# Gate rows of the background conditioning: sum over partitions by one GpSimd instruction instead of four TensorE products

## The chip, the cores and the metric

The kernel runs on one core of a Trainium2 chip. A core has four compute engines that work side by side, each through its own queue in order: TensorE (PE, matrix products into PSUM), VectorE (DVE), ScalarE (ACT) and GpSimd (POOL); a fifth, SyncE (SP), issues the DMA transfers here. The metric is the device time of one execution in microseconds. The kernel before took 2260.77 us (median of three runs, 2260.18 to 2261.73).

## What is computed

Two layers of a diffusion backbone on 256 latent tokens of width 2048, with 256 context tokens beside them in the first layer. Every layer takes six modulation vectors from the conditioning vector c, and two of these are gates:

```python
def ada_mods(cvec, w, b):
    m = jax.nn.silu(cvec) @ w + b          # w is 2048 x 12288
    return jnp.split(m, N_MOD, axis=-1)    # shift, scale, gate; shift, scale, gate

hl = modulate(rms_norm(x, g_norm_mix[layer]), sh1, sc1)
yl = even_mixer(hl, ...) or pool_mixer(hl, ...)
x = x + gt1[:, None, :] * yl
x = x + gt2[:, None, :] * sq_relu_mlp(modulate(rms_norm(x, g_norm_ffn[layer]), sh2, sc2), w_up, w_down)
```

Everything is in float32. A gate multiplies whole columns of an output whose rows (tokens) lie on the 128 partitions, so it must stand in a tile of 128 equal rows.

## The kernel before

The work is a chain of large products: input projections and a gated linear attention with a chunk mixer (the even layer, up to about 550 us), an output projection, a feed-forward of 8192 columns (from about 660 us), a pooling layer (about 1400 to 1545 us) and the second feed-forward. Float32 products are made of parts that TensorE takes at speed: load_w (line 171) loads 1 MB of weights into raw, and for each 1024 columns ScalarE rounds them to hi (line 184) and VectorE makes the rest, lo = raw - hi (line 185), with three buffers each. The groups mma, mmb and mmf multiply hi and lo with the two parts of the activations, xt.

Beside this chain runs the conditioning, in the background. A comp is one vector of 2048 numbers, made by two tasks of 1024 columns each (ada, line 343; ada_task, line 294). A task is 16 chunks: a chunk loads 512 KB of w_ada to araw (line 308), and VectorE adds it, times its number of silu(c), onto acc (line 312), so that acc holds 128 partial sums a column, one in each partition. first (line 299) clears acc by a memset on GpSimd and loads the bias into row 0. last (line 316) sums over the partitions. It splits acc into two parts hi and lo, and then there are two cases. For a shift or scale, products with one-hot columns give rows of numbers, which are transposed to columns. For a gate (row is true), the products with a 128x128 matrix of ones give the sum in every partition at once, 512 columns at a time, and ScalarE copies them from PSUM to the gate tile (line 327). Ten comps, twenty tasks, four gates: eight tasks take the second case.

Chunks are put on a list, bg; pump (line 190) is called after each weight load and takes chunks from it at a rate that plan sets, at a priority below the chain's; need empties the list up to a comp that is now wanted. The tiles acc, araw and the parts share one ring of seven buffers (tag a4, 4 KB a partition). The scheduler of the framework writes each engine's order ahead of time from priorities and its own costs; on the chip each engine follows that order and waits where something isn't ready. GpSimd runs nothing but memsets and the powers of rstd (line 291). The gate tiles of the first gate lie in the ring g4, the others in a pool of four (gate_tile, line 215); residual (line 402) and grow read them.

Of the kernel before, what the change touches and what calls it, by code (L numbers as in the profile page):

```python
# [19 lines left out]
P = 128  # L20
# [130 lines left out]
class Builder:  # L151
# [142 lines left out]
    def ada_task(self, task, dst, row):  # L294

        nc = self.nc
        st = {}

        def first():
            st["acc"] = self.ap.tile([P, 1024], F32, tag="a4", bufs=NA4, name="acc")  # L300
            nc.gpsimd.memset(st["acc"], 0.0)
            nc.sync.dma_start(st["acc"][0:1, :], self.I["bada"][task:task + 1, :])

        def chunk(c):
            if c == 0:
                first()
            raw = self.ap.tile([P, 1024], F32, tag="a4", bufs=NA4, name="araw")
            nc.sync.dma_start(raw, self.I["wada"][task * 16 + c])
            acc = st["acc"]

            with self.tc.issue_after(self.norm) if self.norm is not None else nullcontext():
                nc.vector.scalar_tensor_tensor(acc, raw, self.csil[:, c, 0:1], acc, ALU.mult, ALU.add)  # L312
            if c == KT - 1:
                last()

        def last():
            hi, lo = (self.ap.tile([P, 1024], F32R, tag="a4", bufs=NA4, name="apart") for _ in range(2))
            nc.scalar.copy(hi, st["acc"])
            nc.vector.tensor_sub(lo, st["acc"], hi.bitcast(F32))
            if row:  # L320
                g = self.gate_tile()
                dst.append(g)
                for j in range(2):
                    ps = self.pa.tile([P, 512], F32, tag="ax", name="ps_ada")
                    for i, z in enumerate((hi, lo)):
                        self.mm(ps, self.ones, z[:, 512 * j:512 * j + 512], i == 0, i == 1)
                    nc.scalar.copy(g[:, 512 * j:512 * j + 512], ps)
            else:
                ps = self.pa.tile([P, 512], F32, tag="ax", name="ps_ada")
                rows = self.cp.tile([4, T], F32, tag="crow", bufs=1, name="crow")  # L330
                for j in range(4):
                    for i, z in enumerate((hi, lo)):
                        self.mm(ps[0:4, 0:T], self.hot[:, j], z[:, T * j:T * j + T], j + i == 0, j + i == 4)
                nc.scalar.copy(rows, ps[0:4, 0:T])
                for h in range(2):
                    nc.tensor.transpose(ps[:, T + 4 * h:T + 4 * h + 4], rows[:, h * P:h * P + P], self.ident[0:4, 0:4])
                nc.scalar.copy(dst.rearrange("p (j h) -> p h j", h=2), ps[:, T:T + 8].rearrange("p (h j) -> p h j", h=2))

        for c in range(KT):
            self.bg.append((task // 2, lambda c=c: chunk(c)))  # L340
# [814 lines left out]
```

## Time and profile before

| | us |
|---|---|
| median of three runs | 2260.77 |
| profiled execution, whole | 2260.99 |
| its span, first to last instruction | 2258.9 |
| TensorE busy | 2234.0 (99%) |
| VectorE busy | 1684.9 (75%) |
| ScalarE busy | 1103.0 (49%) |
| GpSimd busy | 36.6 (2%) |

The page shows one profiled execution. Busy time is the time in which an engine had an instruction in work; matmuls overlap, so that the sum of their durations is more than TensorE's busy time, and the step from the start of one to the start of the next tells what one takes. A group of instructions has its count, its busy time, its mean duration, and the idle time of its engine just before it with what ended that idle time. Idle time of an engine that others don't wait for costs nothing.

### The profile page before, as it was taken

The page shows a single profiled execution, that of the slowest core. Times are in us where ns is not written, and L with a number is a line of the kernel's source. Part 1 is how long each engine was busy: PE and PEld are TensorE (multiplying, and loading weights), DVE is VectorE, ACT ScalarE, POOL GpSimd, SP SyncE. Part 2 cuts the span into 40 slices and gives each one's busy share as a digit, 9 for nine tenths or more (in the row PEclk, how much of TensorE's full clock was granted, in tenths as well). Part 3 has the DMA queues.
Part 4 walks back from the last instruction along what each step waited for, and adds up shares of the span by engine and source line. Part 5 has one row for each costly group of instructions (what it writes and reads, how often), then busy time and mean ns, then how long its engine had stood idle before and what let it go on. Part 6 is the DMA issues. An engine that isn't in the chain of part 4 may idle for free. (4 is left out here: it accounts for less than half of the span.)

```text
span 2258.9 us, 31641 instructions
## 1 busy us (share of the span) xinstructions
PE 2234.0 (99%) x12532; PEld 1858.7 (82%) x12532; DVE 1684.9 (75%) x2055; ACT 1103.0 (49%) x1484; POOL 36.6 (2%) x47
## 2 busy tenths in 40 slices
PE   9999999999999999999999999999999999999998
PEld 5677787788888888888888888888888888888887
DVE  5669999998869877787888875769855655556655
ACT  4326466555436545544544545445444444443443
POOL 0000000000000000000000000000000000000000
PEclk9999999999999999999999999999999999999999
DMA  9786776788877888888888875646865555555553
GB/s 384 276 302 220 273 257 241 274 298 299 320 263 285 311 321 304 295 326 311 314 320 316 305 286 207 215 176 248 303 235 193 186 189 199 186 191 186 188 193 122
DMA packets 110636, 582.71 MB, mean 258 GB/s; under 512 B 12292, under 2 KB 12420, under 8 KB 66584
## 3 DMA queue, kind: packets, MB, share of 16 engines
q1 hardware_dynamic: 110488, 580.70, 70.8%
q8 instruction: 98, 1.61, 0.3%
q14 instruction: 50, 0.41, 0.0%
HBM read 578.55 MB, written 2.10 MB: 257 GB/s over the span
## 5 line engine op out<-in xcount | busy, mean ns | idle before, releaser
L184 ACT CAST hi<-raw 128x1024 fp32r<-128x1024 f32 (+1 forms) x701 | 732.9, 1046 | 926.2 <-PE mma L221 463.1
L185 DVE TENSOR_TENSOR lo<-raw,hi 128x1024 fp32r<-128x1024 f32 (+1 forms) x701 | 848.8, 1214 | 410.6 <-ACT hi L184 408.7
L221 PE MATMUL mma<-hi,xt 128*128 128x512 f32 x2800 | 871.5, 390 | 0.1
L221 PE MATMUL mmb<-xt,hi 128*128 128x512 f32 x2304 | 727.3, 396 | 1.1 <-DVE xt L390 0.8
L221 PEld LDWEIGHTS mma<-hi,xt 128*128 128x128 f32 x2800 | 524.6, 188 | 111.0 <-DVE q L281 0.5
L221 PE MATMUL mma<-lo,xt 128*128 128x512 f32 x1400 | 546.2, 390 | 0.8 <-DVE lo L185 0.8
L221 PEld LDWEIGHTS mmb<-xt,lo 128*128 128x128 f32 x2304 | 432.5, 188 | 103.5 <-DVE lo L185 2.5
L221 PE MATMUL mmb<-xt,lo 128*128 128x256 f32 x2304 | 455.0, 278 | 1.4 <-DVE lo L185 1.4
L312 DVE SCALAR_TENSOR_TENSOR acc<-araw,csil,acc 128x1024 f32<-128x1024 f32 x320 | 409.1, 1278 | 49.5 <-DMA araw<-in_wada 47.9
L221 PEld LDWEIGHTS mmb<-xt,hi 128*128 128x128 f32 x2304 | 352.7, 189 | 3.3 <-DVE xt L390 1.0
L221 PEld LDWEIGHTS mma<-lo,xt 128*128 128x128 f32 x1400 | 262.9, 188 | 57.1 <-DVE lo L185 1.5
L221 PE MATMUL mmf<-xt,hi 128*128 128x512 f32 x512 | 165.4, 395 | 0.6 <-ACT fbacc L602 0.5
L221 PEld LDWEIGHTS mmf<-xt,hi 128*128 128x128 f32 x512 | 96.1, 188 | 21.5 <-ACT fbacc L602 0.9
L221 PE MATMUL mmf<-xt,lo 128*128 128x512 f32 x256 | 100.2, 392 | 0.0
L221 PE MATMUL mmn<-hi,xt 128*128 128x256 f32 x416 | 76.0, 283 | 0.0
L221 PEld LDWEIGHTS mmn<-hi,xt 128*128 128x128 f32 x416 | 65.2, 192 | 0.4
L221 PE MATMUL mmn<-lo,xt 128*128 128x256 f32 x208 | 58.9, 283 | 0.0
L221 PEld LDWEIGHTS mmf<-xt,lo 128*128 128x128 f32 x256 | 48.2, 188 | 9.4
L741 ACT COPY both<-kk 128x256 f32<-128x256 f32 x64 | 26.4, 412 | 48.3 <-DVE kk L759 40.2
L390 DVE TENSOR_TENSOR xt<-hup,xt 128x512 fp32r<-128x512 f32 x64 | 43.8, 685 | 6.7 <-ACT xt L389 6.7
L604 DVE TENSOR_TENSOR fbacc<-mmf,fbacc 128x1024 f32<-128x1024 f32 x24 | 29.3, 1220 | 22.0 <-PE mmf L221 21.9
L221 PE MATMUL mmi<-hi,xt 128*128 128x512 f32 x128 | 44.2, 404 | 1.2 <-DVE xt L569 0.6
(187 smaller groups left out, 1341.0 us busy)
## 6 DMA issues: line engine op xcount, KB each, us to landing
araw<-in_wada SPq DMA_DIRECT2D x320, 512.0 KB
raw<-in_w_up SPq DMA_DIRECT2D x128, 1024.0 KB
raw<-in_w_down SPq DMA_DIRECT2D x128, 1024.0 KB
sraw<-in_wada_s SPq DMA_DIRECT2D x56, 512.0 KB
raw<-in_w_out SPq DMA_DIRECT2D x16, 1024.0 KB
raw<-in_w_pool SPq DMA_DIRECT2D x16, 1024.0 KB
raw<-in_w_fb SPq DMA_DIRECT2D x10, 1024.0 KB
raw<-in_w_q SPq DMA_DIRECT2D x8, 1024.0 KB
```

Of the source, the lines that this page charges most:

```text
L184: nc.scalar.copy(hi, raw[:, o:o + w])
L185: nc.vector.tensor_sub(lo, raw[:, o:o + w], hi.bitcast(F32))
L221: self.first_mm = self.nc.tensor.matmul(out, lhsT, rhs, start=start, stop=stop, **kw).ins
L312: nc.vector.scalar_tensor_tensor(acc, raw, self.csil[:, c, 0:1], acc, ALU.mult, ALU.add)
L390: return self.nc.vector.tensor_sub(x[:, :, lo], src, x[:, :, hi].bitcast(F32))
L604: nc.vector.tensor_add(fbacc[h], ps, fbacc[h])
L741: nc.scalar.copy(o.rearrange("p (s j i) -> p j s i", j=2, i=hh), bass.AP(src.tensor, src.offset, [list(src.ap[0]), [st + hh, 2], [seg, ns] ...
```

## The change

In last, a gate's task no longer splits acc and multiplies it with ones. One GpSimd instruction reads acc (128 partitions, 1024 columns), sums over the partitions and writes the sum to all 128 partitions of the gate tile. Shifts and scales are made as before.

```diff
@@ -314,6 +314,11 @@
                 last()
 
         def last():
+            if row:
+                g = self.gate_tile()
+                dst.append(g)
+                nc.gpsimd.partition_all_reduce(g, st["acc"], P, bass.bass_isa.ReduceOp.add)
+                return
             hi, lo = (self.ap.tile([P, 1024], F32R, tag="a4", bufs=NA4, name="apart") for _ in range(2))
             nc.scalar.copy(hi, st["acc"])
             nc.vector.tensor_sub(lo, st["acc"], hi.bitcast(F32))
```

The scheduler writes new orders for all engines. On GpSimd's queue, in the even layer, the piece around the first two gate tasks reads as follows (+ is new, - is gone; acc is the sum tile of a task, orr and vrr are results of rstd, ISA gate<-acc is the new instruction, and ISA alone an entry without operands):

```order
 L301 MEMSET acc 128x1024 x4
+L320 ISA
+L320 ISA gate<-acc 128x1024
+L301 MEMSET acc 128x1024
+L320 ISA gate<-acc 128x1024
+L291 ISA
 L291 TENSOR_TENSOR orr<-oms,mhalf 128x8
-L301 MEMSET acc 128x1024 x3
+L301 MEMSET acc 128x1024 x2
 L291 TENSOR_TENSOR vrr<-vms,mhalf 128x8 x2
```

The memset of the next task stands ahead of a task's sum over partitions, and that of the task after next behind it.

On VectorE's queue, at the end of the first task of the second gate (in the feed-forward of layer 0), the order before was this; the first L312 ends one task's acc, and the pair further down begins the next one's:

```order
L185 TENSOR_TENSOR lo<-raw_7905,hi 128x1024
L312 SCALAR_TENSOR_TENSOR acc<-araw,csil,acc 128x1024
L185 TENSOR_TENSOR lo<-raw_7905,hi 128x1024
L319 TENSOR_TENSOR apart<-acc,apart 128x1024
L185 TENSOR_TENSOR lo<-raw,hi 128x1024 x2
L185 TENSOR_TENSOR lo<-raw_7981,hi 128x1024 x2
L185 TENSOR_TENSOR lo<-raw,hi 128x1024
L312 SCALAR_TENSOR_TENSOR acc<-araw,csil,acc 128x1024 x2
```

Now it is this, at the same place of VectorE's queue:

```order
L185 TENSOR_TENSOR lo<-raw_7883,hi 128x1024
L312 SCALAR_TENSOR_TENSOR acc<-araw,csil,acc 128x1024
L185 TENSOR_TENSOR lo<-raw_7883,hi 128x1024
L185 TENSOR_TENSOR lo<-raw,hi 128x1024 x2
L185 TENSOR_TENSOR lo<-raw_7959,hi 128x1024
L312 SCALAR_TENSOR_TENSOR acc<-araw,csil,acc 128x1024 x2
L185 TENSOR_TENSOR lo<-raw_7959,hi 128x1024
L185 TENSOR_TENSOR lo<-raw,hi 128x1024
L312 SCALAR_TENSOR_TENSOR acc<-araw,csil,acc 128x1024 x2
```

The subtraction of acc is gone, and the next task's additions stand two instructions nearer to the end of this one.

On SyncE's queue the loads behind the same place now read so; what an entry waits for stands in brackets, and Pool_49 is GpSimd's semaphore:

```order
L174 DMA raw_8061<-in_w_up 128x2048 [waits DVE_49]
L308 DMA araw<-in_wada 128x1024 [waits DMAHW2_49]
L308 DMA araw<-in_wada 128x1024 [waits DMAHW4_49,DMAHW3_49]
L174 DMA raw<-in_w_up 128x2048 [waits DVE_49]
L308 DMA araw<-in_wada 128x1024 [waits DMAHW6_49,DMAHW5_49]
L308 DMA araw<-in_wada 128x1024 [waits Pool_49]
L174 DMA raw_8184<-in_w_up 128x2048 [waits DMAHW7_49,DVE_49]
```

The load of the next task's fourth chunk takes the buffer of acc and so waits for GpSimd, ahead of the weights of raw_8184; there are seven such loads behind gate tasks in the whole queue.

## Rows read from the trace of the kernel before

**Rows 1.** Page, span and part 1: busy us (share of the span) xinstructions.

```profile
span 2258.9 us, 31641 instructions
PE 2234.0 (99%) x12532; PEld 1858.7 (82%) x12532; DVE 1684.9 (75%) x2055; ACT 1103.0 (49%) x1484; POOL 36.6 (2%) x47
```

**Rows 2.** Waits of TensorE's matmuls: us in total, times, longest us.

```profile
PE mmb L221 <- DVE lo L185: 1.4, 2, 0.9
```

**Rows 3.** Page, part 5: line, engine, group, busy us, mean ns, idle before.

```profile
L184 ACT CAST hi<-raw 128x1024 fp32r<-128x1024 f32 (+1 forms) x701 | 732.9, 1046 | 926.2 <-PE mma L221 463.1
L185 DVE TENSOR_TENSOR lo<-raw,hi 128x1024 fp32r<-128x1024 f32 (+1 forms) x701 | 848.8, 1214 | 410.6 <-ACT hi L184 408.7
...
L312 DVE SCALAR_TENSOR_TENSOR acc<-araw,csil,acc 128x1024 f32<-128x1024 f32 x320 | 409.1, 1278 | 49.5 <-DMA araw<-in_wada 47.9
```

**Rows 4.** Timeline, second feed-forward: start us, us, engine, line, operation.

```profile
1976.21 1.05 ACT L184 CAST hi<-raw 128x1024 fp32r<-128x1024 f32 x1 [1.25 <-PE mmb L221]
...
1977.30 1.23 DVE L185 TENSOR_TENSOR lo<-raw,hi 128x1024 fp32r<-128x1024 f32 x1 [0.23 <-ACT hi L184]
...
1981.84 1.05 ACT L184 CAST hi<-raw 128x1024 fp32r<-128x1024 f32 x1 [1.75 <-PE mmb L221]
...
1984.60 1.09 PE L221 MATMUL ps_ada<-apart,ones 128*128 128x512 f32 x4
...
1985.53 0.40 PE L221 MATMUL mma<-hi,xt 128*128 128x512 f32 x1
```

**Rows 5.** Tiles apart and gate: ns min/median/max, first and last start us.

```profile
L221 PE MATMUL ps_ada<-apart,ones x32: 388/392/403, 339.0 to 1985.3; 128*128 128x512 f32 x32
L318 ACT CAST apart<-acc x20: 1046/1053/1058, 211.7 to 1652.7; 128x1024 fp32r<-128x1024 f32 x20
L319 DVE TENSOR_TENSOR apart<-acc,apart x20: 1210/1218/1227, 213.0 to 1653.8; 128x1024 fp32r<-128x1024 f32 x20
...
L414 DVE TENSOR_TENSOR rtmp<-mma,gate x24: 678/683/693, 606.6 to 2227.9; 128x512 f32<-128x512 f32 x24
L327 ACT COPY gate<-ps_ada x16: 569/587/599, 339.9 to 1986.5; 128x512 f32<-128x512 f32 x16
```

**Rows 6.** GpSimd's groups, shapes apart: busy us, mean ns, idle before.

```profile
L301 POOL MEMSET acc<- 128x1024 f32 x20 | 19.1, 956 | 1139.9 <-DVE acc L312 904.7 <-PE ps_as L221 120.9 <-DMA araw<-in_wada 114.3
L291 POOL TENSOR_TENSOR vrr<-vms,mhalf 128x8 f32<-128x8 f32 x2 | 5.3, 2636 | 48.6 <-DVE vms L839 26.8 <-DVE oms L804 21.8
...
L291 POOL TENSOR_TENSOR orr<-oms,mhalf 128x8 f32<-128x8 f32 x2 | 3.3, 1638 | 61.5 <-DVE oms L804 61.5
```

**Rows 7.** Timeline of GpSimd and VectorE, 495 to 500 us.

```profile
496.35 1.28 DVE L312 SCALAR_TENSOR_TENSOR acc<-araw,csil,acc 128x1024 f32<-128x1024 f32 x1
...
496.47 2.66 POOL L291 TENSOR_TENSOR vrr<-vms,mhalf 128x8 f32<-128x8 f32 x1 [26.80 <-DVE vms L839]
...
497.55 1.23 DVE L185 TENSOR_TENSOR lo<-raw,hi 128x1024 fp32r<-128x1024 f32 x1
```

**Rows 8.** Stretches: length; PE, PEld, DVE, ACT, POOL busy; PEclk, DMA share, GB/s.

```profile
130.00:550.00 420.00, 412.83 (x2963) 331.94 (x2963) 386.20 (x702) 230.47 (x413) 16.10 (x12) 1.00 0.73 267
660.00:1400.00 740.00, 737.67 (x3902) 628.24 (x3902) 587.77 (x557) 379.02 (x461) 10.69 (x12) 1.00 0.82 297
```

**Rows 9.** Timeline: additions to acc on VectorE, one pair of loads on SyncE.

```profile
308.89 1.27 DVE L312 SCALAR_TENSOR_TENSOR acc<-araw,csil,acc 128x1024 f32<-128x1024 f32 x1
...
849.96 1.28 DVE L312 SCALAR_TENSOR_TENSOR acc<-araw,csil,acc 128x1024 f32<-128x1024 f32 x1 [2.21 <-DMA araw<-in_wada]
...
865.29 1.65 SPq L308 DMA_DIRECT2D araw<-in_wada  x2
...
871.37 1.28 DVE L312 SCALAR_TENSOR_TENSOR acc<-araw,csil,acc 128x1024 f32<-128x1024 f32 x1 [0.51 <-DMA araw<-in_wada]
...
919.18 1.28 DVE L312 SCALAR_TENSOR_TENSOR acc<-araw,csil,acc 128x1024 f32<-128x1024 f32 x1
...
949.00 1.28 DVE L312 SCALAR_TENSOR_TENSOR acc<-araw,csil,acc 128x1024 f32<-128x1024 f32 x1
```

## The prediction

> **What bounds the kernel now.** I read the summary of the engines first. TensorE is busy for 2234.0 of 2258.9 us, and VectorE for three quarters of the span [rows 1]. A busy TensorE could still be one that is often kept waiting for a moment, so the list of its waits comes next: its matmuls waited for a split weight half (lo) 1.4 us in all in the group that waited longest for one [rows 2]. The groups show the other side: ScalarE, which writes the hi halves, sat idle for 926 us before them and was let go mostly by TensorE [rows 3]. So weights are ready ahead of TensorE nearly everywhere, and the end moves with TensorE's own instructions, one for one, as long as VectorE and the loads keep their lead. How large that lead is decides this case.
>
> **The lead of the weights.** A loaded weight tile is split in parts of 1024 columns, hi by ScalarE and then lo by VectorE, with three buffers each. In the feed-forward stage a hi begins every 2.8 us (two steps from 1976.21 to 1981.84) [rows 4], each time when TensorE lets a buffer go. Two other parts are then still ahead of it, so TensorE wants this part near 1976.2 + 2 x 2.8 = 1981.8. Its lo is finished at 1977.30 + 1.23 = 1978.5 [rows 4]. VectorE may therefore be late by 3.3 us before TensorE stands still.
>
> **What is removed.** Eight tasks make a gate half each. Each loses four products with the matrix of ones, one cast, one subtraction and two copies out of PSUM: in all 32 matmuls, 8 of the 20 casts, 8 of the 20 subtractions and 16 copies [rows 5]. A matmul has a duration of 392 ns, but they overlap; what one takes from TensorE is the step to the next. Four begin from 1984.60 on and the next product begins at 1985.53, so a step is 0.233 us [rows 4], and 32 x 0.233 = 7.4 us. They stand between matmuls that hardly wait, so all 7.4 us are on the path. VectorE loses 8 x 1.22 = 9.8 us and ScalarE 8 x 1.05 + 16 x 0.59 = 17.8 us [rows 5]; both were ahead, so I count nothing for them. Two buffers of the ring of seven (the hi and lo of acc) are no longer taken; one, acc itself, is held while the reduce runs.
>
> **What is added: eight reduces on GpSimd.** No row shows one. From below, one pass that reads and one that writes 128x1024, each at the price of a memset of that size, 0.956 us: 1.9 us [rows 6]. From above, a power on 8 columns takes 1.638 us, 0.205 us a column [rows 6], so 1024 columns would take 210 us. Between these far ends I take the memset, since adding is nearer to a pass than to a power: 128 partitions are seven halvings, at one pass each 7 x 0.956 = 6.7 us, at a read and a write each 13.4 us. I take 6.7 us and keep 13.4 us for the range. The Trainium skill, page "GPSIMD Engine Reference", section 3.2, gives 247.7 us for a different cross-partition reduction of [128, 2048]; half of it, an estimate of 124 us, would make the kernel slower by hundreds of microseconds (the last rival). No run here shows it so far.
>
> **What runs beside them.** GpSimd is idle for nearly the whole span [rows 1]: its own time costs nothing by itself. But the reduce reads SBUF while VectorE does, and the trace has two places where such a pair meets. The power vrr takes 2.66 us at 496.47, when VectorE has just begun an accumulation of 1.28 us with two inputs from SBUF (496.35) [rows 7]; the two vrr take 2.636 us in the mean, and orr, of the same shape, 1.638 us [rows 6]. So GpSimd waited about 1.0 us, until VectorE's instruction was over, and got in before the next one; the lo at 497.55 kept its 1.23 us [rows 7], but there GpSimd had only eight columns to read. One side waits for the other, then, for an instruction at a time. With 1024 columns to read I expect the other side of it: the next VectorE instruction with two SBUF inputs, and all behind it in VectorE's queue, stands still until the reading is over. In the order of the changed kernel that is at once a lo, since four of them follow the last accumulation of a task. The rule stands in the Trainium skill, page "SBUF — State Buffer", section "Who interferes with whom": the pair of ports that the two share is locked by whoever comes first, for its whole instruction, also against a VectorE instruction with two SBUF inputs. The trace agrees for the half that it shows, GpSimd's 1.0 us; with the rule the sum is the one below, without it that of the first rival.
>
> Let the hold be h = 6.7 us. In the six feed-forward cases VectorE is 79% busy (587.77 of 740 us) [rows 8]. The first lo caught would on average have begun half a part, 1.4 us, after the hold began, and I put 0.5 us of other work before it: late by h - 1.4 + 0.5 = 5.8 us, less the lead of 3.3: TensorE stands for 2.5 us, six times 15.0. In the two cases of the even layer VectorE is 92% busy (386.20 of 420 us) [rows 8]; there I take the lo as due at once and 0.7 us of work before it: h + 0.7 - 3.3 = 4.1 us, twice 8.2. Together 23.2 us, or in general 8h - 30.4.
>
> **Queues.** GpSimd's queue gets six entries without operands (three at line 320, three at line 291), which I read as changes of the program that it runs. No row prices one. Each stands where GpSimd has nothing due for some 10 us: the first directly behind the memset for the second gate task, which the first task's last additions don't wait for, and what comes next, the sum of the first, is ready only at 308.89 + 1.27 = 310.2 [rows 9]. I cost them at nothing; a long one would cost what it exceeds that gap by. Behind a reduce stands the memset of the task after next, wanted after a whole further task. On SyncE's queue one load now waits for the reduce, since it takes over the buffer of acc, and weight loads queue behind it: tightest for the fourth chunk behind the task that ends at 849.96 + 1.28 = 851.2 [rows 9]. Loads land 4.8 us after issue (the second of the pair from 865.29 begins near 866.6, its sum at 871.37) [rows 9], and in the new order its sum comes near 866, by four lo's at the pace of 2.8 us and three sums: a reduce over 10 us makes VectorE wait, one over 13 us (the lead) TensorE too. At 6.7 us: nothing. The gates are wanted later: the first use of any is at 606.6 [rows 5], some 300 us after the first task's sum.
>
> **The sum**, against the profiled execution, 2260.99 us (2258.9 of span and 2.1 around it, 0.2 above the median of the runs): 2260.99 - 7.4 + 23.2 = 2276.8, said as 2277 us. In general 2260.99 + 8h - 37.8: it breaks even at h = 4.7 us, and ends at 2330 with 13.4 us. A measurement of this kernel can tell about 0.2%, 4.5 us, from no change; slower by that needs an h of 5.3 us.
>
> **Rivals.** *Faster: GpSimd gives way.* If the reduce reads in short pieces between VectorE's instructions, VectorE keeps its pace and only the 7.4 us count: 2253.6 us. For it: the lo of 1.23 us beside a running power [rows 7]. The reduce is then stretched: lo and accumulation take 848.8 + 409.1 = 1257.9 of 2258.9 us, 56% [rows 3], so 6.7 becomes 6.7 / 0.44 = 15 us, which at the one tight load costs 15 - 13 = 2 us: 2255.6. This side wins below a hold of 4.7 us. I give it 0.33, with 2251 to 2258 us. *Much slower: a slow reduce.* At a price per column like the power's, 210 us, loads behind seven of the eight wait. The usual slack is that of the sixth chunk behind: from 919.18 + 1.28 = 920.5 to 949.00 [rows 9], less 4.8 to land, plus the lead, 27 us. That makes 7 x (210 - 27) = 1281 us more, some 3535 us with the 7.4 off. Against it: a power is the dearest thing that GpSimd does here. By the Trainium skill's figure, page "GPSIMD Engine Reference", 124 us as an estimate, the same sum would give 7 x 97 = 679 us more. I give it 0.05.
>
> **How the numbers follow.** The forecast has 0.62, and its own range is 2262 to 2300 us (h from 4.9 to 9.6). Of it 0.48 lies above 0.2% slower, 0.09 within and 0.05 faster; of the first rival 0.24 is faster, 0.06 the same, 0.03 slower; the last is slower. That is faster 0.29, same 0.15, slower 0.56. The range runs from 2251 (the first rival, with a microsecond or two more from shorter queues) to 2300; left out are the slow reduce, 0.05, holds above 9.6 us, about 0.1, and a little below.
>
> **What would show it.** Eight GpSimd instructions that write gate, of 5 to 10 us. If I am right, at each of them one VectorE instruction with two SBUF inputs is longer than its 1.2 us by several microseconds, or has a gap before it, and the next matmuls wait for lo by 2 to 4 us; TensorE's waits for lo grow from a few us to some 20. If lo keeps 1.22 us there and TensorE has no new gaps, the first rival holds. A load of araw that waits past 10 us for a gate shows the stretched reduce. Wrong altogether I would be if the program changes held up rstd at a layer's start, or if the 32 matmuls had covered work that now comes late.

## The result, and the profile after

The changed kernel takes 2273.88 us (median of five runs, 2272.46 to 2276.08) where the kernel before takes 2260.77 beside it: a ratio of 1.006, with an interval of 1.005 to 1.0071. It is slower by 13 us. The forecast was 2277. The number is nearly right, but two of its terms are wrong by some 10 us each, in opposite directions, and that is what the experiments are about.

The page of the changed kernel, span and part 1, against [rows 1]:

```profile
span 2274.3 us, 31571 instructions
PE 2235.9 (98%) x12500; PEld 1856.3 (82%) x12500; DVE 1702.6 (75%) x2047; ACT 1088.7 (48%) x1460; POOL 90.9 (4%) x55
```

This profiled execution took 2276.08 us as a whole, so 15.1 us more than that of before. TensorE has 32 matmuls less and is busy for longer; VectorE has eight instructions less and is busy for 18 us longer. Part 5 of the page (busy us, mean ns, idle before) shows where VectorE's comes from, against [rows 3], and what the new instruction takes:

```profile
L185 DVE TENSOR_TENSOR lo<-raw,hi 128x1024 fp32r<-128x1024 f32 (+1 forms) x701 | 868.6, 1244 | 387.2 <-ACT hi L184 382.0
...
L312 DVE SCALAR_TENSOR_TENSOR acc<-araw,csil,acc 128x1024 f32<-128x1024 f32 x320 | 417.5, 1305 | 71.9 <-DMA araw<-in_wada 70.4
...
L320 POOL PARTITION_ALL_REDUCE gate<-acc x8 | 56.2, 7024 | 167.9 <-DVE acc L312 152.7
```

A reduce takes 7.02 us; the forecast had 6.7. The same 701 lo and the same 320 accumulations are 28.2 us longer in all. The means hide how: the view of the tile lo (duration in ns, least, median and most) has the same median as before, and a longest one of 5551.

```profile
L185 DVE TENSOR_TENSOR lo<-raw,hi x701: 679/1224/5551, 23.6 to 2258.4; 128x1024 fp32r<-128x1024 f32 x173, 128x512 fp32r<-128x512 f32 x3
```

The timeline of the changed kernel around the first reduce, in the even layer (start us, us, engine, line, operation, and in brackets the idle time before and what ended it):

```profile
310.24 6.49 POOL L320 PARTITION_ALL_REDUCE gate<-acc  x1 [15.29 <-DVE kk L764]
...
310.66 5.55 DVE L312 SCALAR_TENSOR_TENSOR acc<-araw,csil,acc 128x1024 f32<-128x1024 f32 x1
316.13 0.28 DVE L764 TENSOR_TENSOR kk<-kk,pyr 128x128 f32<-128x128 f32 x1
...
318.04 0.41 ACT L746 COPY both<-kk 128x256 f32<-128x256 f32 x1 [5.81 <-DVE kk L764]
...
320.81 0.43 PE L221 MATMUL ps_sc<-both 128*32 128x64 f32 x16 [3.80 <-ACT both L746]
...
867.89 6.92 POOL L320 PARTITION_ALL_REDUCE gate<-acc  x1 [9.01 <-DVE acc L312]
...
869.68 4.62 DVE L185 TENSOR_TENSOR lo<-raw,hi 128x1024 fp32r<-128x1024 f32 x1 [0.86 <-ACT hi L184]
```

An accumulation of 1.27 us takes 5.55. The small multiplications kk and qg behind it in VectorE's queue wait, ScalarE's copy waits for kk for 5.81 us, and TensorE stands for 3.80 us before the small matmul ps_sc. In the feed-forward stage (the last two rows) a lo is caught in the same way, 4.62 us for 1.22, and no matmul there waits for long. The list of TensorE's waits (us in total, times, longest) says the same of the whole execution:

```profile
PE ps_o L221 <- ACT st L788: 6.4, 6, 4.5
PE ps_sc L221 <- ACT both L746: 5.1, 5, 3.8
PE ps_mx L221 <- issue: 3.7, 1, 3.7
...
PE mma L221 <- DVE lo L185: 1.9, 4, 0.7
PE mmb L221 <- DVE lo L185: 1.8, 4, 0.5
```

The waits for lo are 3.7 us in all now, not some 20; before they were 2.2 (1.4 in mmb [rows 2] and 0.8 in mma). The new waits are those of the even layer's small matmuls. Where TensorE stands there, its granted clock falls behind it. In the stretches of 5 us (length, busy us of PE, PEld, DVE, ACT, POOL, then the granted clock) it is 0.70 behind the first reduce and 0.50 at 510 us, as means of the two levels, 1.2 and 2.4 GHz; the kernel before has 1.00 throughout 130 to 550 us [rows 8]. A mean of 0.70 over 5 us is 3 us at the lower level. Counted in this way the changed kernel spends 3.4 us there behind each of the first two reduces and 6.8 us from 510 us on, and at the lower level the same product takes twice the time. That is how TensorE can be busy for longer with 32 products less.

```profile
315.00:320.00 5.00, 2.00 (x86) 1.42 (x84) 5.00 (x11) 0.71 (x2) 1.73 (x1) 1.00 0.46 134
320.00:325.00 5.00, 4.19 (x47) 3.63 (x47) 5.00 (x11) 4.96 (x9) 0.00 (x0) 0.70 0.89 342
...
510.00:515.00 5.00, 3.85 (x11) 3.31 (x12) 3.28 (x9) 1.05 (x1) 0.67 (x1) 0.50 0.85 349
515.00:520.00 5.00, 5.00 (x26) 4.34 (x26) 3.81 (x7) 0.56 (x1) 0.00 (x0) 0.84 0.61 221
```

**Where the time came from.** Every kernel here makes 701 hi casts, so the n-th cast of one can be set against the n-th of another. The table gives how much later than in the kernel before the cast that stood at 298.6, 490.6, 608.6, 1179.9 and 2230.1 us began (from the timelines of the profiled executions). The first two steps are the even layer, the last two the rest with its feed-forward stages. The kernels below the first row are those of the next section.

| kernel | 298.6 | 490.6 | 608.6 | 1179.9 | 2230.1 |
|---|---|---|---|---|---|
| changed | -0.2 | 6.9 | 17.4 | 17.4 | 15.3 |
| e1, gate 0 on TensorE | 0.2 | -0.3 | -0.2 | -2.2 | -4.2 |
| e2, gate 0 alone on GpSimd | 0.3 | 8.8 | 13.5 | 13.9 | 13.1 |
| e3, no reading | 1.0 | -1.3 | 3.0 | -2.0 | -3.6 |
| e4, reduces twice | 0.3 | 18.3 | 25.2 | 39.5 | 45.0 |
| e5, pieces | 0.1 | 6.0 | 10.3 | 5.4 | 3.6 |
| e6, gate 0 later | -0.1 | 8.9 | 12.2 | 10.1 | 8.5 |
| e7, gate 0 on TensorE, rest in pieces | 1.1 | 0.3 | 0.3 | -3.3 | -6.2 |
| e8, as e7, no reading | 0.0 | 0.0 | 0.1 | -4.8 | -7.7 |
| e9, gate 0 put off | 2.5 | -0.9 | 14.9 | 10.2 | 8.7 |
| e10, put off, behind the memset | 0.8 | -1.5 | 7.5 | 3.1 | 2.4 |

Each row is one execution, and a median differs from it by up to 3.5 us (the changed kernel was profiled at 2276.08 for a median of 2273.88, e1 at 2256.89 for 2260.36, e5 at 2264.32 for 2267.02, e6 at 2269.19 for 2272.65). A difference of 2 or 3 us between two rows is a hint and not a proof.

The changed kernel loses 17.6 us in the even layer, with two reduces, and wins 2.0 behind it, with six. There are two parts to the loss: 7.1 us up to 490 us, where the reduces are, and 10.5 between 490 and 608, where there is none.

### The profile page after: what moved, and what is told of

Its sections match the earlier page's. It is cut to its first block, busy times and chain, and to the rows that moved or that the text cites. A ratio compares the mean times of both kernels' runs of the same rounds, so it can differ in the third digit from the quotient of the medians.

```text
span 2274.3 us, 31571 instructions
## 1 busy us (share of the span) xinstructions
PE 2235.9 (98%) x12500; PEld 1856.3 (82%) x12500; DVE 1702.6 (75%) x2047; ACT 1088.7 (48%) x1460; POOL 90.9 (4%) x55
## 4 chain that ended last, share of the span: by engine, by line
PE 80%; DVE 9%; DMA 6%; issue 3%; ACT 2%; POOL 0%; SPq 0%; DVEq 0%; POOLq 0%; ACTq 0%
PE mma L221 35%; PE mmb L221 31%; DMA araw<-in_wada 4%; PE mmf L221 3%; PE mmn L221 3%; DVE lo L185 3%; DVE acc L312 2%; PE mmi L221 2%; PE ps_as L221 1%; ACT hi L184 1%; PE ps_warm L221 1%; DVE qg L764 1%; DVE kk L764 1%; DMA raw<-in_w_u 1%; PE ps_o L221 1%
## 5 line engine op out<-in xcount | busy, mean ns | idle before, releaser
L185 DVE TENSOR_TENSOR lo<-raw,hi 128x1024 fp32r<-128x1024 f32 (+1 forms) x701 | 868.6, 1244 | 387.2 <-ACT hi L184 382.0
L312 DVE SCALAR_TENSOR_TENSOR acc<-araw,csil,acc 128x1024 f32<-128x1024 f32 x320 | 417.5, 1305 | 71.9 <-DMA araw<-in_wada 70.4
L320 POOL PARTITION_ALL_REDUCE gate<-acc x8 | 56.2, 7024 | 167.9 <-DVE acc L312 152.7
L301 POOL MEMSET acc<- 128x1024 f32 x20 | 19.1, 956 | 1024.5 <-DVE acc L312 721.5
```

The costliest lines, as they stand in the source:

```text
L185: nc.vector.tensor_sub(lo, raw[:, o:o + w], hi.bitcast(F32))
L320: nc.gpsimd.partition_all_reduce(g, st["acc"], P, bass.bass_isa.ReduceOp.add)
```

## The experiments

**Which reduces cost: e1 and e2.** Each kernel gives one half of the gate tasks back to TensorE.

```diff
         def last():
-            if row:
+            if row and task > 1:
```

> Gate 0's two tasks, the ones in the even layer, go back to TensorE's products with the matrix of ones; the six gate tasks of the feed-forward stages stay on GpSimd. Theory (the loss arises in the even layer, where a held VectorE instruction keeps the small multiplications, and so the small matmuls, waiting): the +17.3 us up to 600 us go away whole, and from there on the casts run as in the changed kernel, 1.9 us ahead in all: 2260.8 - 1.9 = about 2259 us, at 310 to 600 us the same start times as before. Rival (the prediction's own account: 2.5 us lost at every reduce of the feed-forward stages, less what the products cost there): six times 2.5 less 24 x 0.233 = 9.4 us slower, about 2270 us. Rival (the loss comes with the program that GpSimd must change, wherever the reduces stand): six of eight parts stay, about 2271 us.

Measured: 2260.36 us against 2261.53, ratio 0.9998 (0.9987 to 1.0009). The even layer's loss is gone whole, as the table shows. The runs of this kernel spread from 2256.59 to 2269.0, so that the 2 to 4 us that the feed-forward stages win in the profiled executions can't be told from nothing in its times.

```diff
         def last():
-            if row:
+            if row and task <= 1:
```

> The other half: only gate 0's two tasks, in the even layer, go to GpSimd; the six of the feed-forward stages stay on TensorE. Theory (even layer): the +17.3 us stand at 600 us as in the changed kernel and nothing is won or lost behind them: 2260.8 + 17.3 = about 2278 us, 4 us above the changed kernel. Rival (a loss at each reduce): two of eight parts, about 2264 us.

Measured: 2274.46 us, ratio 1.0057 (1.0045 to 1.007), that is, the whole loss of the changed kernel. The even layer costs it, and not each reduce alike. It is 4 us less than I had expected: up to 490 us this kernel, whose engines run the even layer in the same order, loses about as much as the changed one (8.5 us for 7.1), but between 490 and 608 only 4.7.

**Whether it is the reading: e3.** GpSimd is kept busy, and the order of VectorE, ScalarE and TensorE is that of the changed kernel, but GpSimd hardly reads.

```diff
-                nc.gpsimd.partition_all_reduce(g, st["acc"], P, bass.bass_isa.ReduceOp.add)
+                add = bass.bass_isa.ReduceOp.add
+                nc.gpsimd.partition_all_reduce(g[:, 0:8], st["acc"][:, 0:8], P, add)
+                for _ in range(6):
+                    nc.gpsimd.memset(g, 0.0)
+                nc.gpsimd.partition_all_reduce(g[:, 0:8], st["acc"][:, 0:8], P, add)
```

> Each reduce is replaced by a reduce of 8 columns, six memsets of the gate tile, and another reduce of 8 columns: GpSimd is busy for about as long (6 x 0.96 us and two short ones), at the same place in its queue, with the order of the other engines as in the changed kernel, but it reads next to nothing from SBUF. The gate sum is left out but for 8 columns. Theory (VectorE's instructions with two SBUF inputs are held while GpSimd reads 128x1024): no accumulation and no lo is stretched, and the loss goes: 2260.8 - 7.4 = about 2253 to 2257 us. Rival (the new order of the loads and of VectorE's queue in the even layer costs it, whatever GpSimd does): +17 stays there, 2270 to 2274 us. Rival (writing holds VectorE like reading): as the changed kernel, 2274 us, with stretched instructions still in the trace.

Measured: 2258.29 us, ratio 0.9987 (0.9978 to 0.9996), a little above the theory's 2253 to 2257 and far below both rivals. Behind the first gate task GpSimd is busy for longer than with the reduce (8.9 us for 6.5), and no lo and no accumulation is longer than before (the longest accumulation is 1.29 us). Of this kernel, the timeline of GpSimd and the view of the tile lo:

```profile
311.47 0.79 POOL L321 PARTITION_ALL_REDUCE gate<-acc  x1 [15.29 <-DVE kk L768]
312.32 6.01 POOL L323 MEMSET gate<- 128x1024 f32 x6
318.44 2.11 POOL L324 PARTITION_ALL_REDUCE gate<-acc  x1
```

```profile
L185 DVE TENSOR_TENSOR lo<-raw,hi x701: 680/1224/1228, 23.6 to 2239.4; 128x1024 fp32r<-128x1024 f32 x173, 128x512 fp32r<-128x512 f32 x3
```

So the hold comes with the reduce of 1024 columns, and six memsets, each of which writes as many, hold nothing. The Trainium skill, page "SBUF — State Buffer", section "Who interferes with whom", says that a VectorE instruction with two SBUF inputs contends with a GpSimd instruction that reads SBUF, not with one that only writes it; both traces agree. That it is the reading in the reduce, and not something else that the reduce alone does, no run here separates. But e3 also shows a part that is not the hold. In the even layer it is 2.3 us ahead at 490 us and 2.0 behind at 608: 4.3 us are lost between, in an order of instructions that it shares with the changed kernel, without any reduce of more than 8 columns. The four kernels e2, e3, e5 and e10 lose 4.2 to 4.7 us there up to 540 or 608 us. I take it for the price of the new order, which no run undid by itself: in the traces the scheduler has put two lo and one accumulation more between the first statistics of the chunk mixer and their end, vms, for which its power and its matmuls wait: 5.5 us before (490.69 to 496.23), 9.7 in e3 (488.71 to 498.40).

**How long a hold is: e5 and e4.** In e5 the sum is made in four pieces, in e4 it is made twice.

```diff
-                nc.gpsimd.partition_all_reduce(g, st["acc"], P, bass.bass_isa.ReduceOp.add)
+                for o in range(0, 1024, 256):
+                    nc.gpsimd.partition_all_reduce(g[:, o:o + 256], st["acc"][:, o:o + 256], P, bass.bass_isa.ReduceOp.add)
```

> The same reduce in four pieces of 256 columns each. Theory (VectorE is held for one GpSimd instruction at a time, and may go on between two): no VectorE instruction is stretched by more than some 2 us, one or more instructions get in between the pieces, and the even layer loses less than half of its 17.3 us: 2256 to 2266 us. Rival (each piece holds VectorE anew and the pieces are no shorter, since a fixed part of a reduce dominates): four holds of 3 to 5 us, 2285 us or more. Rival (the order of the loads is what costs): as the changed kernel, 2272 to 2275 us.

Measured: 2267.02 us, ratio 1.0024 (1.0015 to 1.0033). No VectorE instruction is stretched by 2 us any more, as the theory said, but the time lies a microsecond above its range, and the even layer loses 10.2 us in the table, not less than half of 17.3. The timeline of GpSimd and VectorE of this kernel at the first gate task:

```profile
310.62 9.13 POOL L321 PARTITION_ALL_REDUCE gate<-acc  x4 [15.30 <-DVE kk L765]
...
311.04 2.12 DVE L312 SCALAR_TENSOR_TENSOR acc<-araw,csil,acc 128x1024 f32<-128x1024 f32 x1
313.08 1.18 DVE L765 TENSOR_TENSOR kk<-kk,pyr 128x128 f32<-128x128 f32 x1
...
315.52 1.18 DVE L765 TENSOR_TENSOR kk<-kk,pyr 128x128 f32<-128x128 f32 x1
...
318.02 1.18 DVE L765 TENSOR_TENSOR kk<-kk,pyr 128x128 f32<-128x128 f32 x1
```

At this task each piece catches one instruction, for 0.85 to 0.90 us: the accumulation 2.12 for 1.27, a small multiplication 1.18 for 0.28. Four make 3.5 us, against 4.28 of the whole reduce (5.55 less 1.27), and VectorE is free between them. In the even layer that helps little up to 490 us (5.9 us lost for 7.1); as I read the trace, VectorE has no time to spare there and kk is what is caught. Behind it the six reduces in pieces win 6.7 us, where the whole ones win 2.0.

```diff
-                nc.gpsimd.partition_all_reduce(g, st["acc"], P, bass.bass_isa.ReduceOp.add)
+                for _ in range(2):
+                    nc.gpsimd.partition_all_reduce(g, st["acc"], P, bass.bass_isa.ReduceOp.add)
```

> Every reduce is done twice in a row (the same result written again). Theory (a hold lasts some 4.6 us of a reduce, and TensorE pays what of it is beyond the lead of the weights of 3.3 us): two holds make 9.2 us in some 13 us; with 0.9 us that the first caught instruction saves and 0.8 us that VectorE's spare time gives back, 4.2 us are lost at each of the six reduces of the feed-forward stages instead of about 0.5, and 4 to 8 us more at each of the even layer's: 2274 + 22 + 8 to 16 = 2304 to 2312 us. Rival (the weights are further ahead than the prediction's lead of 3.3 us, so the feed-forward stages swallow two holds as well): only the even layer grows, 2282 to 2290 us.

Measured: 2305.73 us, ratio 1.019 (1.0174 to 1.0206), inside the forecast. Two holds stand behind each other, the second on a small multiplication of 0.28 us, and in the feed-forward stages TensorE now does wait for lo. The timeline of VectorE and TensorE's waits of this kernel:

```profile
311.00 5.55 DVE L312 SCALAR_TENSOR_TENSOR acc<-araw,csil,acc 128x1024 f32<-128x1024 f32 x1
...
318.01 4.62 DVE L765 TENSOR_TENSOR kk<-kk,pyr 128x128 f32<-128x128 f32 x1
```

```profile
PE mmb L221 <- DVE lo L185: 10.8, 9, 4.2
...
PE mma L221 <- DVE lo L185: 7.6, 7, 3.6
```

Set against e3, which has no holds, the six feed-forward reduces cost 6.6 - 2.0 = 4.6 us with one hold each and 19.8 + 6.6 = 26.4 with two, for which I had worked out 6 x 4.2 = 25 from a hold of 4.6 us and the prediction's lead of 3.3. A hold that is little longer than the lead costs little (0.8 us each), and a second one behind it most of its length: 26.4 less 4.6 is 3.6 us each, of a stretch of 4.3.

**The feed-forward stages by themselves: e7 and e8.** Gate 0 goes back to TensorE as in e1, and the other six are made as in e5 (e7) or as in e3 (e8).

> Gate 0's two tasks on TensorE again, the six of the feed-forward stages on GpSimd in four pieces of 256 columns. Theory (a hold that is shorter than the lead of the weights costs nothing, and the even layer is as before): all 24 x 0.233 = 5.6 us come through, 2261.5 - 5.6 = about 2256 us, and 2 to 3 us below the kernel with whole reduces in these six places. Rival (the holds of the feed-forward stages cost nothing anyway, whole or in pieces): no difference from that kernel, about 2259 to 2260 us. Rival (four fixed parts of a piece cost more than the shorter holds bring): above it, 2262 us or more.

> Gate 0's two tasks on TensorE again; in the six of the feed-forward stages GpSimd does a reduce of 8 columns, six memsets and another of 8 columns in place of the reduce, so that it is busy as long and reads next to nothing. Their gate sum is left out but for 8 columns. This prices the removed products by themselves. Theory: 24 x 0.233 = 5.6 us below the kernel before and nothing lost, about 2256 us. Rival (the products stood where TensorE would have waited for weights or loads anyway, so that less than all of it comes through): 2258 to 2261 us.

Measured: e7 2254.57 us against 2260.55, ratio 0.9976 (0.9967 to 0.9985); e8 2254.1 us, ratio 0.9967 (0.9955 to 0.9979). The removed products are worth what the step of 0.233 us said, 5.6 us, and a little more, and pieces of 256 columns leave nearly all of it. e7 is below e1 by more than the 2 to 3 us expected (0.9976 against 0.9998), but e1's runs spread too widely to make much of that. **e7 computes all that the kernel before does and is faster than both kernels.** Its pieces take 2.48 us each in the mean, 9.7 for a task, on an engine that has nothing else to do there:

```profile
L321 POOL PARTITION_ALL_REDUCE gate<-acc x24 | 57.9, 2482 | 128.0 <-DVE acc L312 128.0
```

**Other places for gate 0's holds: e6, e9 and e10.** First, memsets in front of the two reduces, to make them start later:

```diff
+                for _ in range({0: 20, 1: 32}.get(task, 0)):
+                    nc.gpsimd.memset(g, 0.0)
                 nc.gpsimd.partition_all_reduce(g, st["acc"], P, bass.bass_isa.ReduceOp.add)
```

> The changed kernel, but GpSimd writes zeros to the gate tile 20 times before the first reduce of gate 0 and 32 times before the second, so that these two begin some 19 and 31 us later, behind the run of small multiplications that the small matmuls wait for; the six others are untouched. Theory (what a hold costs in the even layer hangs on what VectorE has next in its queue): the two holds still stretch a VectorE instruction by 3 to 5 us, but the small matmuls wait less and the even layer loses 4 to 10 us instead of 17: 2260 to 2267 us. Rival (VectorE is 92% busy there, so a hold of 4 us is lost wherever it falls): no better, 2272 to 2276 us. Rival (the accumulator that is held longer keeps a load waiting, and VectorE with it): worse, above 2277 us.

Measured: 2272.65 us, ratio 1.0057 (1.004 to 1.0073), but the kernel did not do what it was made for. The memsets need nothing from acc and ran ahead of its last additions, so that the first reduce began at 324.45 us only, and it caught the last of the very multiplications that it was to miss (4.83 us for two, normally some 0.5):

```profile
324.45 6.34 POOL L322 PARTITION_ALL_REDUCE gate<-acc  x1 [8.69 <-DMA araw<-in_wada]
...
324.71 4.83 DVE L766 TENSOR_TENSOR qg<-qg,pyr 128x128 f32<-128x128 f32 x2
```

So the number, though it is that of the first rival, tests neither theory nor rival. It tells only that a hold at another time of that layer costs as much. The next one puts the sums off for good: ScalarE copies the two accumulators to the gate tiles, and the sums are made in place, in pieces, when the last task before their use is done (task 8; sum_parts is the loop of e5, and last_rstd the last power).

```diff
+                if task <= 1:
+                    nc.scalar.copy(g, st["acc"])
+                    self.late = getattr(self, "late", []) + [g]
+                    return
+                self.sum_parts(g, st["acc"])
                 return
+            if task == 8:
+                with self.tc.issue_after(self.last_rstd):
+                    for g in self.late:
+                        self.sum_parts(g, g)
```

> All eight sums on GpSimd, in pieces of 256 columns, but gate 0's are put off: ScalarE copies each finished accumulator to its gate tile (one instruction of about 1 us each), and the two sums are done in place behind the last power of the even layer, near 525 us, where no run of small multiplications stands on VectorE; the order of the other engines is nearly that of the changed kernel. Theory (a hold costs what VectorE's next work keeps waiting, not the hold itself): the even layer loses what the new order costs without any reading, 3 us by the profile of the kernel that reads next to nothing, and 0 to 3 us for the holds at 525 to 545 us; the feed-forward stages win 6 us: 2260.6 + 3 + 0 to 3 - 6 = 2257 to 2260 us. Rival (VectorE is so busy in the even layer that held time is lost wherever it falls): 7 us more for the pieces, as where they stood before, about 2265 us. Rival (without the two holds the order costs nothing): 2252 to 2254 us, the fastest of all.

Measured: 2269.99 us, ratio 1.0041 (1.0028 to 1.0055): none of the three. Up to 540 us it runs as e3 does (2.8 us behind), and then it loses 12 us at once. The timeline there, of GpSimd, SyncE, VectorE and TensorE, shows a queue:

```profile
524.52 1.64 POOL L291 TENSOR_TENSOR orr<-oms,mhalf 128x8 f32<-128x8 f32 x1
534.26 15.48 POOL L296 PARTITION_ALL_REDUCE gate<-gate  x8 [8.09 <-issue]
549.61 1.02 POOL L305 MEMSET acc<- 128x1024 f32 x1
...
550.66 0.24 SPq L306 DMA_DIRECT2D acc<-in_bada  x1
551.01 0.33 SPq L174 DMA_DIRECT2D raw<-in_w_u  x1
...
552.12 1.28 DVE L316 SCALAR_TENSOR_TENSOR acc<-araw,csil,acc 128x1024 f32<-128x1024 f32 x1 [9.36 <-DMA acc<-in_bada]
...
553.72 0.48 PE L833 MATMUL ps_ro<-ident,sgt 128*128 128x128 f32 x1 [10.43 <-DVE sgt L825]
```

The memset of the next accumulator stands behind the eight pieces. The load of the bias row waits for the memset, and the weight load behind it on SyncE waits too. VectorE's first addition of the next task waits 9.36 us, and what stands behind that, sgt, is what TensorE needs. From 550 to 555 us TensorE's granted clock is 0.50. The row of the pieces also shows a price that the kernel before had not shown: after the power ended at 526.16 us GpSimd waited for nothing but its own start for 8.09 us. Before the first reduce behind a power stands one of the entries without operands that the prediction read as a change of program.

The last kernel only moves the pieces behind that memset (issue_after names the memset of task 9 in place of the power).

> As the kernel with gate 0's sums put off, but the eight pieces stand in GpSimd's queue behind the memset of the next accumulator (task 9's, near 532 us) and not ahead of it; nothing due stands behind them for 100 us. Theory (the 12 us lost there at 540 to 553 us came from that memset: it waited for a start of the first piece that was 8.1 us late and for 15.5 us of pieces, the load of the bias row waited for it, and the weight load behind that in SyncE's queue too): all 12 us come back, and the kernel takes 2270 - 12 = about 2258 us. Rival (they came from the held VectorE instructions, eight of 0.9 us in a busy stretch): no better than 2268 us. Rival (gate 0 is still waited for at 606 us): 2260 us or more, with a new wait of the first residual addition there.

Measured: 2261.94 us against 2262.08, ratio 0.9999 (0.999 to 1.0008). The queue was the larger part: of the 12 us 7.4 came back. The late start costs nothing now, though it is as long (8.33 us), since nothing due stands behind it. So the theory named the larger part, and its time is 4 us too low. The third rival's number fits, but not its reason: no residual addition waits for gate 0. The rest is a hold again, as the second rival had it for the whole, on the small multiplications sgt: 3.0 us of standing, and a clock of 0.66 behind it (545 to 550 us). The timeline and one row of TensorE's waits:

```profile
525.52 0.95 POOL L305 MEMSET acc<- 128x1024 f32 x1
534.81 16.50 POOL L296 PARTITION_ALL_REDUCE gate<-gate  x8 [8.33 <-issue]
...
547.80 3.22 DVE L825 SCALAR_TENSOR_TENSOR sgt<-o_all,orr,sgt 128x128 f32<-128x128 f32 x5
```

```profile
PE ps_ro L833 <- DVE sgt L825: 3.2, 2, 3.0
```

Gate 0 is better left with TensorE: its products cost 1.9 us, and every way tried to take them off cost more than that.

## Why the number was right and its steps were not

**Removed products: right, a little low.** 32 x 0.233 = 7.4 us were forecast. The feed-forward stages' 24 bring 6.6 to 7.7 us in e3 and e8, where nothing is held, for 5.6 forecast; gate 0's eight bring 2.3 in e3 up to 490 us, for 1.9.

**The reduce: right; the hold: right in kind, too long.** 6.7 us were estimated from the memset [rows 6], 7.02 are the mean. No run shows that a reduce goes in seven passes, so that the estimate hit is luck. That a VectorE instruction with two SBUF inputs is stretched is seen at all eight reduces. The step that failed is h = 6.7 us, the hold taken as long as the reduce. Three of the eight caught instructions are 4.28 to 4.33 us longer (the two accumulations of the even layer 5.55 for 1.27, the longest lo 5551 for 1224 ns). The five others are lo's that began later in the reduce, most of them because they waited for their hi, and are 3.2 to 3.7 us longer. The instruction at 310.66 us is let go 4.7 us after the reduce began (310.66 + 5.55 - 1.27 = 314.94), if its own 1.27 us come behind the hold; in the same way of counting all eight are let go 1.7 to 1.8 us before the reduce ends. So the rule of the Trainium skill, page "SBUF — State Buffer", section "SBUF: two separate sides", that whoever starts first gets the shared pair of ports for the whole instruction, agrees in kind but not in its length here: 4.7 of 6.5 us. The spans of GpSimd's own instructions are the roughest in a profile; the 4.3 us are VectorE's.

**The six feed-forward reduces: mis-sized by that h.** 15.0 us were forecast, 4.6 are found (changed kernel against e3). The formula itself held: the six caught lo's are 3.6 us late in the mean, where the prediction had 6.7 - 1.4 = 5.3, and 6 x (3.6 + 0.5 - 3.3) = 4.8; with two holds 25 were worked out for 26.4 measured. The lead of 3.3 us from [rows 4] fits both, though no run measures it by itself.

**The two even-layer reduces: right in size, wrong in the path.** 8.2 us were forecast. Up to 490 us the changed kernel is 7.1 + 2.3 = 9.4 us behind e3, some 4.7 us a hold, and e4 with four holds 20.3. But TensorE did not wait for lo. The short work on VectorE that I had put at 0.7 us is the link that counts: kk, ScalarE's copy, the small matmul. At the second reduce it is st, the copy that ps_o waits for. That chain has no three buffers, so there is no lead of 3.3 us to take off; in its place the hold is shorter, and TensorE's clock falls behind each gap. That can be counted another way: between the casts of the table's first two columns TensorE is idle for 11.3 us, in e3 for 4.8, with 1481 matmuls in both; and two times 3.4 us at the lower clock cost up to 3.4 us of work (an estimate from the granted clock). That is 6.5 + 3.4 = 9.9 for 9.4. That the errors of the forecast cancel here is luck.

**The order: missing in the sum.** I counted nothing for what VectorE and ScalarE lose in work, and looked at no more of the new order than its queues. In the even layer 4.3 us are lost in the new order without a hold (e3), and in the changed kernel another 6.1 between 490 and 608 us. That execution shows a weight load that landed late: ScalarE waited for it, VectorE's lo for that, and with it the statistics of the chunk mixer, until TensorE stood for 3.71 us. The timeline of SyncE, ScalarE and TensorE of the changed kernel:

```profile
494.40 0.33 SPq L174 DMA_DIRECT2D raw<-in_w_v  x1
...
502.38 2.01 ACT L184 CAST hi<-raw 128x1024 fp32r<-128x1024 f32 x2 [3.82 <-DMA raw<-in_w_v]
...
511.15 0.77 PE L221 MATMUL ps_mx<-wsp,vg 128*128 128x128 f32 x2 [3.71 <-issue]
```

e2, in the same order, lost 5.7 us less there. From 490 to 520 us its TensorE stands for 2.1 us and the granted clock stays at 1.00; in the changed kernel it stands for 3.7 us and then runs at the lower clock up to some 517 us (the stretches of 5 us in the section on the result). At half the pace that is some 2.7 us of work (an estimate), so the clock took more than the longer standing did. What made the load late was not tried and stays open.

**The queues.** The late start that I put down to the change of program is 8.1 to 8.3 us where it is seen best (e9, e10), within the gap of some 10 us in which the prediction saw it hidden. In the changed kernel it shows once, behind the second reduce, which ends at 366.62 us: the timeline of VectorE and GpSimd has the power orr begin at 375.01, 6 us after its input oms was done.

```profile
368.78 0.16 DVE L809 TENSOR_SCALAR oms<-ostat 128x8 f32<-128x8 f32 x1
375.01 1.68 POOL L291 TENSOR_TENSOR orr<-oms,mhalf 128x8 f32<-128x8 f32 x1 [8.39 <-DVE acc L312]
```

It costs nothing there, since orr is first used at 469.2 us. The loads behind a reduce cost nothing, as forecast: at 7 us no araw load held TensorE up in the feed-forward stages. e9 shows what the same queue costs when 24 us stand in it.

**The sum.** By these steps: products -2.3 - 6.6, holds 9.4 and 4.6, order 4.3 and 6.1, together 15.5; the cast at 2230 us is 15.3 + 0.2 = 15.5 us later. These steps are differences of the table's rows, so that they add up is no test of them, and they are those of an execution 2.2 us above the median. The forecast had -7.4 + 15.0 + 8.2. It came near because 10 us too much for the feed-forward stages stood against 10 us of order that it did not have, and that is luck too. The first rival's mechanism did not show: VectorE was held at all eight reduces. But it is what pieces come near to: with them (e7) the products' gain does come through.

## What to carry to other kernels

An engine that reads SBUF in the shadow of VectorE is not free though it is idle: price the hold on VectorE's next two-input instruction, against the lead of whatever that feeds, and do it anew for each stage, since the chain of small operations here had no lead. Cutting the reading into pieces of less than the lead made it nearly free in the feed-forward stages; in the even layer it did not. And where a change lets a scheduler reorder a stage that is near its limit, compare the orders around its tightest wait, and what stands behind the moved work in its new queue, before counting removed work as gain.

## What the chip showed that I had not expected

The hold is not the reduce: 4.3 us of stretching in a reduce of 6.5, and 0.85 to 0.90 in a piece of 256 columns that takes 2.4 in the mean (e5). It catches small instructions as well as large ones: a multiplication of 128x128, 0.28 us, took 4.62 (e4). Nor were those with two SBUF inputs the only ones: beside the pieces of e5 a VectorE instruction with one input of 128x8 took 1.06 us, for 0.16 in the changed kernel (the oms above); why was not tried. The row is from VectorE's timeline in e5:

```profile
366.74 1.06 DVE L810 TENSOR_SCALAR oms<-ostat 128x8 f32<-128x8 f32 x1
```

GpSimd is held up as well: with a lo in work when it began, a reduce of the changed kernel took 6.92 to 7.02 us, and in one case with a second lo right behind it 8.15, for 6.49 and 6.61 in the even layer. And the first partition sum behind a power started 8.1 to 8.3 us late.
